# Moving 64-byte offsets from the moving to the stationary operand of 256-column products

## The chip, the cores and the metric

The kernel runs on one core of one Trainium2 chip. The metric is the device time of one execution in microseconds, as the median of several runs. A profile is one more execution, recorded by the hardware profiler.

## The reference, cut to what matters

The reference is three transformer layers on a sequence of 256 rows of width 1024, all in float32: a layer with two kinds of windowed attention, a layer with retention, each followed by a feed-forward block, and a hybrid layer with three attention branches.

```python
def _mlp(x, norm_g, w1, w2):                       # w1 [1024, 4096], w2 [4096, 1024]
    h = _rmsnorm(x, norm_g)
    return jnp.square(jax.nn.relu(h @ w1)) @ w2
...
a = jnp.einsum('bhid,bhjd->bhij', qc, kc) * dmask      # retention, 8 heads of 128
o = jnp.einsum('bhij,bhjv->bhiv', a, vc) + ...
```

## The kernel before

Every large product is done in float32r, split in two parts: an operand is hi + lo, and a product is three TensorE products, hi times hi, hi times lo and lo times hi (`mm3`, or three calls of `mm`). A TensorE product loads a stationary operand of 128 columns (LDWEIGHTS, the engine row PEld) and then streams a moving operand through it. Products whose moving operand has 512 columns are those of `panel` (a block of activations stationary, 512 columns of weights moving), of `proj` and of `mlp_out`. Products with 256 moving columns are of three kinds:

- `panel_T`, the first half of a feed-forward block: 128 columns of weights are stationary (`wh[:, fs]`, `wl[:, fs]`), all 256 rows of the transposed input xT move (`xh[:, k, :]`, `xl[:, k, :]`). A panel is 96 such products (4 blocks of 128 columns, 8 blocks of depth, 3 parts); there are 8 panels in each of the two feed-forward stages.
- the 16 heads of the first mixer (`even_head`): the values va or vb are stationary, the probabilities ph and pl move.
- the 8 heads of the retention mixer (`head` in `_odd`): for the scores the keys are stationary and the queries move; for the output the decayed scores ah and al are stationary and the values vv move.

Weights stream from memory all the time. SyncE's queue brings blocks of 1 MB into `raw`, ScalarE rounds half a block to `whi` (`w_hi`), VectorE subtracts to get `wlo` (`w_lo`); both are rings of WB = 5 buffers in the pool `wp`, used for all weights in order. A planner (`drive`) with modelled costs decides the order in which the tasks' instructions are written out; a half may be split at most LOOK = 3 halves ahead of the one in use. All tiles that TensorE reads lie at multiples of 512 bytes, with one exception: in the feed-forward stages the tile xT begins 64 bytes later (`xT_tiles(16)`, 16 floats). In the other stages xT is at a multiple of 512 bytes as well (`xT_tiles()`).

The pools of a stage are opened when the stage begins and given back at its end, so that the next stage's tiles lie where those of the last lay. The pool `wp` stands through the whole kernel.

Of the kernel before, what the change touches and what calls it, by code (L numbers as in the profile page):

```python
# [8 lines left out]
F32 = mybir.dt.float32  # L9
F32R = mybir.dt.float32r  # L10
# [5 lines left out]
P = 128  # L16
S = 256
D = 1024
NT = 2
# [18 lines left out]
def vap(ap, dims):  # L38

    return bass.AP(ap.tensor, ap.offset, [ap.ap[0]] + [list(d) for d in dims])  # L40


class Pools:

    def __init__(self, tc, ctx, name):
        self.lines = ctx.enter_context(tc.tile_pool(name=name, bufs=1))
        self.rest = ctx.enter_context(tc.tile_pool(name=name + "_s", bufs=1))

    def tile(self, shape, dt, **kw):
        n = 4
        for d in shape[1:]:
            n *= d
        return (self.rest if n % 512 else self.lines).tile(shape, dt, **kw)


class Task:
# [6 lines left out]
class Kernel:  # L65
# [25 lines left out]
    def __init__(self, ctx, tc, aps, taps=None):  # L91
        self.tc, self.nc, self.aps, self.ctx = tc, tc.nc, aps, ctx
        self.smallp = ctx.enter_context(tc.tile_pool(name="small", bufs=1))
        self.smallp.tile([P, PAD], F32, name="pad")
        self.mainp = ctx.enter_context(tc.tile_pool(name="main", bufs=1))
        self.wp = ctx.enter_context(tc.tile_pool(name="wp", bufs=1))
        self.wp.tile([P, 128 - 32], F32, name="padw")
        self.ps = ctx.enter_context(tc.tile_pool(name="ps", bufs=1, space=PSUM))
        self.now = 0.0
        self.free = {"T": 0.0, "A": 0.0, "V": 0.0, "P": 0.0, "D": 0.0}  # L100
        self.ready, self.used, self.touch = {}, {}, {}
        self.tasks, self.seq, self.cur = [], 0, None
        self.res = {}
        self.banks = [0.0] * 8
        self.ev = {}


    def spawn(self, gen, delay=0.0, prio=1):
# [311 lines left out]
    def w_parts(self, n):  # L420

        w = self.wseq[n // 2][1]
        return [slice(0, w), slice(w, 2 * w)] if n < self.FINE else [slice(0, 2 * w)]

    def w_hi(self):
        for n in range(2 * len(self.wseq)):
            self.cur.prio = lambda: self.w_prio(n, 2.3)
            yield ("if", lambda: n < len(self.wfree) + self.WB and n <= self.hcur + self.LOOK and n // 2 in self.wraw)
            if n >= self.WB:
                yield ("at", self.wfree[n - self.WB])  # L430
            m = 2 * self.wseq[n // 2][1]
            raw = self.wraw[n // 2][:, (n % 2) * m:(n % 2 + 1) * m]
            hi = self.wp.tile([P, 1024], F32R, name="whi", tag="whi", bufs=self.WB)
            self.whi[n] = hi
            for i, c in enumerate(self.w_parts(n)):
                yield from self.act(hi[:, c], raw[:, c], AF.Copy)
                self.fire(("hi", n, i))

    def w_lo(self):
        for n in range(2 * len(self.wseq)):  # L440
            self.cur.prio = lambda: self.w_prio(n, 1.3)
            yield ("ev", ("hi", n, 0))
            m = 2 * self.wseq[n // 2][1]
            raw = self.wraw[n // 2][:, (n % 2) * m:(n % 2 + 1) * m]
            hi = self.whi[n]
            lo = self.wp.tile([P, 1024], F32R, name="wlo", tag="wlo", bufs=self.WB)
            self.whalf[n] = (hi, lo)
            parts = self.w_parts(n)
            for i, c in enumerate(parts):
                yield ("ev", ("hi", n, i))  # L450
                t = yield from self.vtt(lo[:, c], raw[:, c], hi[:, c].bitcast(F32), ALU.subtract)
                self.fire(("w", n, i))
            if len(parts) == 1:
                self.fire(("w", n, 1))
            if n % 2 == 1:
                del self.wraw[n // 2]
                self.rawfree.append(t)
                self.w_dma()
# [155 lines left out]
            yield from post(t, ms)  # L614
        return [ss[0], ss[1], [], [], fin]

    def xT_tiles(self, at=0):

        xT = self.mainp.tile([P, 16 * S + 32], F32R, name="xT", tag="xT", bufs=1)
        return [xT[:, at + i * 8 * S:at + (i + 1) * 8 * S].rearrange("p (k q) -> p k q", k=8) for i in range(2)]  # L620


    def heads_T(self, src, dst, t, key, scale=1.0):
# [13 lines left out]
    def split_T(self, src, hi, lo, k0, t, key, scale=None):  # L637

        n = src.shape[1] // P
        yield ("rdy", src)  # L640
        yield ("acq", "bank", 1)
        ps = self.bank()
        yield ("op", "T", [], [src])
        for i in range(n):
            self.transpose(ps[:, i * P:(i + 1) * P], src[:, i * P:(i + 1) * P])
        pv = ps[:, :n * P].rearrange("p (i q) -> p i q", i=n)
        tk = slice(t * P, (t + 1) * P)
        end = yield from self.split(hi[:, k0:k0 + n, tk], lo[:, k0:k0 + n, tk], pv, scale)
        self.done(ps)
        self.fire(key, at=end)  # L650

# [215 lines left out]
    def _even(self, pool):  # L867
# [61 lines left out]

        qTa = pool.tile([P, 4, S], F32, name="qTa", tag="qTa")  # L930
        kTa = pool.tile([P, 1, S], F32, name="kTa")
        va = [[pool.tile([P, 256], F32R, name=f"va{n}{t}") for n in "hl"] for t in range(NT)]


        def pads():
# [2 lines left out]
        self.spawn(pads(), 12.0, self.LOW)  # L938
        qTb = pool.tile([P, 4, S], F32, name="qTb", tag="qTb")
        kTb = pool.tile([P, 4, S], F32, name="kTb")  # L940
        vb = [[pool.tile([P, 768], F32R, name=f"vb{n}{t}") for n in "hl"] for t in range(NT)]
        oT = [[pool.tile([P, 4, S], F32R, name=f"o{n}0") for n in "hl"], []]
        self.res["pT"], self.res["tab"] = 2, 2

# [111 lines left out]
    def mlp_input(self, i, gcol):  # L1056
        self.r2 = [None] * 2
        for t in range(NT):
            self.ev.pop(("r2", t), None)

        def post(t, ms):
            self.r2[t] = self.mt([P, 1], f"r2{t}", bufs=2)
            yield from self.vrecip(self.r2[t], ms)
            self.fire(("r2", t))
        self.st = self.stats(post)
        self.xT = self.xT_tiles(16)

    def mlp(self, i):
        with self.tc.tile_pool(name=f"mlp{i}", bufs=1) as pool:
            yield from self._mlp(pool, i)  # L1070

    def _mlp(self, pool, i):
        key = f"m{i}"
# [80 lines left out]
    def _odd(self, pool):  # L1154
# [6 lines left out]
        a, u, b, s2 = (scr[:, 16 * i:16 * i + 16] for i in range(4))  # L1161
# [20 lines left out]
        self.res["nat"] = 2  # L1182
        self.res["rhd"] = 2

        def qk_task(hp, qk):
            def task(t, ps):
                yield ("acq", "nat", 1)
                nat = pool.tile([P, 512], F32, name="nat", tag="nat", bufs=2)
                yield from self.act(nat, ps, AF.Copy)
                self.done(ps)  # L1190
                yield from self.split_T(nat, qk[0], qk[1], 0, t, ("rqk", hp, t))
                self.give("nat")
            return task

        def v_task(hp, vv):
            def task(t, ps):
                yield ("ev", ("st", "o", t))
                end = yield from self.split(vv[t][0], vv[t][1], ps, vs[t])
                self.done(ps)
                self.fire(("rv", hp, t), at=end)  # L1200
            return task
# [13 lines left out]
        def head(hp, hh, qk, vv, sg):  # L1215
# [3 lines left out]
            dt = pool.tile([P, 384], F32, name="dt", tag="dt", bufs=2)  # L1219
# [4 lines left out]
            ps = self.bank()  # L1224
            yield ("op", "T", [], [])
            for jt in range(2):
                js = slice(jt * P, (jt + 1) * P)
                self.mm3(ps[:, jt * S:(jt + 1) * S], qk[0][:, 2 + hh, js], qk[1][:, 2 + hh, js], qk[0][:, hh, :],
                         qk[1][:, hh, :], True, True)
            at = pool.tile([P, 512], F32, name="at", tag="at", bufs=2)  # L1230
            yield from self.vtt(at.rearrange("p (j i) -> p j i", j=2), ps.rearrange("p (j i) -> p j i", j=2),
                     vap(dt[:, P:P + S], [[-P, 2], [1, S]]), ALU.mult)
            self.done(ps)
            ah = pool.tile([P, 512], F32R, name="ah", tag="ah", bufs=2)
            al = pool.tile([P, 512], F32R, name="al", tag="al", bufs=2)
            yield from self.split(ah, al, at)
            yield ("rdy", al)
            yield ("ev", ("rv", hp, 0), ("rv", hp, 1))
# [47 lines left out]
            end = yield from self.split(uT[0][:, ks, :], uT[1][:, ks, :], un.rearrange("p (k q) -> p k q", k=2))  # L1286
# [6 lines left out]
        self.res["rset"] = 2  # L1293
        for hp in range(4):
            yield ("acq", "rset", 1)
            qk = [pool.tile([P, 4, S], F32R, name=n, tag=n, bufs=2) for n in ("qkh", "qkl")]
            vv = [[pool.tile([P, 512], F32R, name=n, tag=n, bufs=2) for n in (f"vh{t}", f"vl{t}")]
                  for t in range(NT)]
            sg = [pool.tile([P, 512], F32, name=f"sg{t}", tag=f"sg{t}", bufs=2) for t in range(NT)]
            yield from self.panel(self.xT, "xo", qk_task(hp, qk), tmajor=hp == 0)  # L1300
            for hh in range(2):
                self.spawn(head(hp, hh, qk, vv, sg), hh * 4.0)
            yield from self.panel(self.xT, "xo", v_task(hp, vv))
            yield from self.panel(self.xT, "xo", g_task(hp, sg))
# [446 lines left out]
```

## Time and profile before

| what | value |
|---|---|
| median of 3 runs | 1014.18 us (1013.54 to 1014.5) |
| the profiled execution | 1014.55 us, its span from first to last instruction 1012.8 us |
| TensorE (PE) busy | 1000.0 us, 5602 products |
| weight load (PEld) busy | 860.1 us |
| VectorE (DVE) busy | 689.5 us |
| ScalarE (ACT) busy | 536.1 us |
| granted TensorE clock, mean | 0.994 |

The span is the time from the first to the last instruction of the program; the 1.75 us beside it lie around them. A busy time is the union of an engine's instructions. Products are pipelined: a product's recorded duration is longer than the distance to the next product's start, so the cost of one product in a run is read from the starts, not from the durations.

### The profile page before, as it was taken

The page shows a single profiled execution, that of the slowest core. Times are in us where ns is not written, and L with a number is a line of the kernel's source. Part 1 is how long each engine was busy: PE and PEld are TensorE (multiplying, and loading weights), DVE is VectorE, ACT ScalarE, POOL GpSimd, SP SyncE. Part 2 cuts the span into 40 slices and gives each one's busy share as a digit, 9 for nine tenths or more (in the row PEclk, how much of TensorE's full clock was granted, in tenths as well). Part 3 has the DMA queues.
Part 4 walks back from the last instruction along what each step waited for, and adds up shares of the span by engine and source line. Part 5 has one row for each costly group of instructions (what it writes and reads, how often), then busy time and mean ns, then how long its engine had stood idle before and what let it go on. Part 6 is the DMA issues. An engine that isn't in the chain of part 4 may idle for free.

```text
span 1012.8 us, 14238 instructions
## 1 busy us (share of the span) xinstructions
PE 1000.0 (99%) x5602; PEld 860.1 (85%) x5602; DVE 689.5 (68%) x1133; ACT 536.1 (53%) x817; POOL 39.5 (4%) x44
## 2 busy tenths in 40 slices
PE   9989999999999999999999999999999999999997
PEld 7878889999998888888889999998878788888885
DVE  6997667555556977777667545556769756576774
ACT  7766646444445655656446444445554553454453
POOL 1340000000000000000000000000100000000000
PEclk9989999999999999999999999999999999999999
DMA  9734245555554544443545555553625435543531
GB/s 333 231 112 159 84 166 203 178 202 182 197 204 153 195 166 155 172 171 129 205 166 191 187 206 172 203 207 112 213 83 172 161 136 195 193 172 128 195 125 42
DMA packets 27108, 173.66 MB, mean 171 GB/s; under 512 B 3168, under 2 KB 3424, under 8 KB 7584
## 3 DMA queue, kind: packets, MB, share of 16 engines
q1 hardware_dynamic: 25344, 168.05, 47.2%
q0 software_dynamic: 1120, 4.06, 1.7%
q8 instruction: 44, 0.72, 0.3%
q10 hardware_dynamic: 576, 0.64, 0.2%
q14 instruction: 24, 0.20, 0.1%
HBM read 171.69 MB, written 1.05 MB: 171 GB/s over the span
## 4 chain that ended last, share of the span: by engine, by line
PE 95%; DVE 2%; DMA 1%; ACT 1%; issue 0%; POOLq 0%; ACTq 0%; DVEq 0%
PE bank L326 91%; PE bank L336 4%; DMA x<-in_x 1%; DVE p L273 1%; DVE tab L259 0%; DMA cols<-in_cols 0%; ACT p L246 0%; DVE pl L251 0%; DVE p L259 0%; DVE den L251 0%; DVE wlo L251 0%; DVE st L283 0%; DVE qn L251 0%; ACT whi L246 0%; ACT nraw L246 0%
## 5 line engine op out<-in xcount | busy, mean ns | idle before, releaser
L251 DVE TENSOR_TENSOR wlo<-raw,whi 128x1024 fp32r<-128x1024 f32 (+1 forms) x324 | 384.9, 1191 | 187.9 <-ACT whi L246 183.0
L246 ACT ACTIVATE whi<-raw 128x1024 fp32r<-128x1024 f32 (+1 forms) x324 | 333.3, 1032 | 239.5 <-PE bank L326 233.8
L326 PE MATMUL bank<-whi,xT 128*128 128x512 f32 (+2 forms) x1184 | 378.7, 390 | 0.7 <-ACT whi L246 0.4
L326 PEld LDWEIGHTS bank<-whi,xT 128*128 128x128 f32 x1184 | 221.1, 189 | 45.7 <-issue 3.0
L326 PE MATMUL bank<-wlo,xT 128*128 128x512 f32 (+2 forms) x592 | 227.1, 384 | 0.0
L326 PE MATMUL bank<-xT,whi 128*128 128x256 f32 x1024 | 182.1, 280 | 0.0
L326 PEld LDWEIGHTS bank<-xT,whi 128*128 128x128 f32 x1024 | 157.3, 187 | 1.1
L326 PE MATMUL bank<-xT,wlo 128*128 128x256 f32 x512 | 142.9, 279 | 0.0
L326 PEld LDWEIGHTS bank<-wlo,xT 128*128 128x128 f32 x592 | 112.0, 189 | 18.8
L326 PE MATMUL bank<-whi,hh 128*128 128x512 f32 x256 | 100.3, 392 | 0.0
L326 PE MATMUL bank<-whi,hl 128*128 128x512 f32 x256 | 99.8, 390 | 0.0
L326 PE MATMUL bank<-wlo,hh 128*128 128x512 f32 x256 | 99.6, 389 | 0.0
L326 PEld LDWEIGHTS bank<-xT,wlo 128*128 128x128 f32 x512 | 96.2, 188 | 0.0
L326 PEld LDWEIGHTS bank<-whi,hl 128*128 128x128 f32 x256 | 48.0, 188 | 10.4
L326 PEld LDWEIGHTS bank<-wlo,hh 128*128 128x128 f32 x256 | 48.1, 188 | 9.5
L326 PEld LDWEIGHTS bank<-whi,hh 128*128 128x128 f32 x256 | 48.1, 188 | 9.3
L246 ACT ACTIVATE p<-p,nm 128x256 f32<-128x256 f32 (+1 forms) x64 | 30.2, 473 | 27.1 <-DVE nm L273 26.9
L251 DVE TENSOR_TENSOR h<-h 128x512 f32<-128x512 f32 x32 | 22.0, 688 | 18.1 <-ACT h L246 18.1
L246 ACT ACTIVATE h<-bank 128x512 f32<-128x512 f32 x32 | 18.8, 587 | 28.6 <-PE bank L326 28.6
L246 ACT ACTIVATE hh<-h 128x512 fp32r<-128x512 f32 x32 | 20.2, 632 | 19.6 <-DVE h L251 19.6
L251 DVE TENSOR_TENSOR hl<-h,hh 128x512 fp32r<-128x512 f32 x32 | 22.0, 688 | 11.2 <-ACT hh L246 11.2
L326 PE MATMUL bank<-whi,uh 128*128 128x512 f32 x64 | 25.2, 393 | 0.0
(241 smaller groups left out, 1117.3 us busy)
## 6 DMA issues: line engine op xcount, KB each, us to landing
raw<-in_w_mlp_in SPq DMA_DIRECT2D x32, 1024.0 KB, 4.7
raw<-in_w_mlp_out SPq DMA_DIRECT2D x32, 1024.0 KB, 4.8
raw<-in_w_in SPq DMA_DIRECT2D x32, 1024.0 KB, 4.9
raw<-in_w_in_o SPq DMA_DIRECT2D x24, 1024.0 KB, 4.7
raw<-in_w_out_o SPq DMA_DIRECT2D x8, 1024.0 KB, 4.7
raw<-in_w_in_e SPq DMA_DIRECT2D x6, 1024.0 KB, 5.5
raw<-in_w_up SPq DMA_DIRECT2D x6, 1024.0 KB, 4.9
raw<-in_w_mem SPq DMA_DIRECT2D x4, 1024.0 KB, 4.8
```

The costliest lines, as they stand in the source:

```text
L246: self.nc.scalar.activation(out, in_, func, scale=scale, **kw)
L251: self.nc.vector.tensor_tensor(out, a, b, op=op)
L273: self.nc.vector.tensor_tensor_reduce(out, a, b, scale, init, op0, op1, acc)
L326: self.nc.tensor.matmul(out, lhsT, rhs, start=start, stop=stop, skip_group_check=shared)
L336: self.nc.tensor.transpose(out, in_, self.ident)
```

## The change

The 64 bytes are taken from the moving operand and given to the stationary one, in all three kinds of 256-column products:

- `xT_tiles` gives two tiles, each at a multiple of 512 bytes, in all stages.
- The weights of `w_mlp_in` get rings of their own (`mhi`, `mlo`, five buffers each, tiles of 1024 + 32 floats used from float 16 on) in a pool `mpool` that lives as long as the feed-forward stage. The weights of all other products, `w_mlp_out` among them, stay in `wp`. A half of `w_mlp_in` that is split before the stage has been opened still goes to `wp`.
- The values va and vb of the first mixer and the decayed scores ah and al of the retention mixer lie 64 bytes past a boundary (`half`), in a third pool `mid` of the mixer.
- In the retention mixer, queries and keys share a tile: the queries stay at its start, the keys begin at float 2 * 256 + 16 (`KO`).

The number of instructions of every engine and their shapes stay as they were.

```diff
+def halfway(pool, n, dt, **kw):
+    return pool.tile([P, n + 32], dt, **kw)[:, 16:16 + n]
...
+    def half(self, n, dt, **kw):
+        return halfway(self.mid, n, dt, **kw)
...
-        self.wp.tile([P, 128 - 32], F32, name="padw")
...
+    def w_tile(self, part, n):
+        if self.mpool and self.wseq[n // 2][0].startswith("w_mlp_in"):
+            return halfway(self.mpool, 1024, F32R, name="m" + part, tag="m" + part, bufs=self.WB)
+        return self.wp.tile([P, 1024], F32R, name="w" + part, tag="w" + part, bufs=self.WB)
...
-            hi = self.wp.tile([P, 1024], F32R, name="whi", tag="whi", bufs=self.WB)
+            hi = self.w_tile("hi", n)
...
-            lo = self.wp.tile([P, 1024], F32R, name="wlo", tag="wlo", bufs=self.WB)
+            lo = self.w_tile("lo", n)
...
-    def xT_tiles(self, at=0):
-        xT = self.mainp.tile([P, 16 * S + 32], F32R, name="xT", tag="xT", bufs=1)
-        return [xT[:, at + i * 8 * S:at + (i + 1) * 8 * S].rearrange("p (k q) -> p k q", k=8) for i in range(2)]
+    def xT_tiles(self):
+        return [self.mt([P, 8, S], n, F32R) for n in ("xh", "xl")]
...
-        va = [[pool.tile([P, 256], F32R, name=f"va{n}{t}") for n in "hl"] for t in range(NT)]
+        va = [[pool.half(256, F32R, name=f"va{n}{t}") for n in "hl"] for t in range(NT)]
...
-        vb = [[pool.tile([P, 768], F32R, name=f"vb{n}{t}") for n in "hl"] for t in range(NT)]
+        vb = [[pool.half(768, F32R, name=f"vb{n}{t}") for n in "hl"] for t in range(NT)]
...
-        self.xT = self.xT_tiles(16)
+        self.xT = self.xT_tiles()
...
-        with self.tc.tile_pool(name=f"mlp{i}", bufs=1) as pool:
+        with self.tc.tile_pool(name=f"mlp{i}", bufs=1) as pool, self.tc.tile_pool(name=f"mlp{i}_h", bufs=1) as self.mpool:
             yield from self._mlp(pool, i)
+        self.mpool = None
...
+        KO = 2 * S + 16
...
-                yield from self.split_T(nat, qk[0], qk[1], 0, t, ("rqk", hp, t))
+                yield from self.split_T(nat, *(vap(v[:, t * P:], [[KO, 2], [S, 2], [1, P]]) for v in qk), None, t,
+                                        ("rqk", hp, t))
...
-                self.mm3(ps[:, jt * S:(jt + 1) * S], qk[0][:, 2 + hh, js], qk[1][:, 2 + hh, js], qk[0][:, hh, :],
-                         qk[1][:, hh, :], True, True)
+                js = slice(KO + hh * S + jt * P, KO + hh * S + (jt + 1) * P)
+                qs = slice(hh * S, (hh + 1) * S)
+                self.mm3(ps[:, jt * S:(jt + 1) * S], qk[0][:, js], qk[1][:, js], qk[0][:, qs], qk[1][:, qs], True, True)
...
-            ah = pool.tile([P, 512], F32R, name="ah", tag="ah", bufs=2)
-            al = pool.tile([P, 512], F32R, name="al", tag="al", bufs=2)
+            ah = pool.half(512, F32R, name="ah", tag="ah", bufs=2)
+            al = pool.half(512, F32R, name="al", tag="al", bufs=2)
...
-            qk = [pool.tile([P, 4, S], F32R, name=n, tag=n, bufs=2) for n in ("qkh", "qkl")]
+            qk = [pool.mid.tile([P, 4 * S + 32], F32R, name=n, tag=n, bufs=2) for n in ("qkh", "qkl")]
```

## Rows read from the trace of the kernel before

**Rows 1.** The page: span, busy time of the engines, and the chain that ended last.
```profile
span 1012.8 us, 14238 instructions
...
PE 1000.0 (99%) x5602; PEld 860.1 (85%) x5602; DVE 689.5 (68%) x1133; ACT 536.1 (53%) x817; POOL 39.5 (4%) x44
...
PE 95%; DVE 2%; DMA 1%; ACT 1%; issue 0%; POOLq 0%; ACTq 0%; DVEq 0%
```

**Rows 2.** Windows: the two feed-forward stages; window, length, then busy (count) by engine.
```profile
150.40:319.80 169.40, 169.40 (x1112) 155.43 (x1112) 98.77 (x104) 84.38 (x99) 0.00 (x0) 1.00 0.54 189
...
531.00:700.80 169.80, 169.80 (x1114) 155.68 (x1113) 98.75 (x104) 84.33 (x99) 0.00 (x0) 1.00 0.54 187
```

**Rows 3.** Groups by form, TensorE: the 256-column products; count, busy us, mean ns.
```profile
L326 PE MATMUL bank<-xT,whi 128*128 128x256 f32 x1024 | 182.1, 280 | 0.0
...
L326 PE MATMUL bank<-xT,wlo 128*128 128x256 f32 x512 | 142.9, 279 | 0.0
...
L326 PE MATMUL bank<-vh,al 128*128 128x256 f32 x32 | 9.1, 283 | 0.0
...
L326 PE MATMUL bank<-ph,vah 128*128 128x256 f32 x16 | 4.7, 291 | 0.0
...
L326 PE MATMUL bank<-qkh,qkl 128*128 128x256 f32 x16 | 4.5, 283 | 0.0
```

**Rows 4.** Timeline, TensorE, first feed-forward stage: start us, duration us, what.
```profile
204.92 0.40 PE L326 MATMUL bank<-xT,whi 128*128 128x256 f32 x2
...
216.23 0.40 PE L326 MATMUL bank<-whi,hh 128*128 128x512 f32 x1
...
227.15 0.40 PE L326 MATMUL bank<-xT,whi 128*128 128x256 f32 x2
```

**Rows 5.** Timeline, TensorE, a retention head: 24 products with 256 columns between two with 512.
```profile
355.76 0.28 PE L326 MATMUL bank<-vh,ah 128*128 128x256 f32 x1
355.88 0.28 PE L326 MATMUL bank<-vl,ah 128*128 128x256 f32 x1
...
358.64 0.40 PE L326 MATMUL bank<-whi,xT 128*128 128x512 f32 x1
```

**Rows 6.** Timeline, TensorE, a head of the first mixer: 12 products after a 512-column one.
```profile
48.49 0.28 PE L326 MATMUL bank<-ph,vah 128*128 128x256 f32 x1
48.60 0.28 PE L326 MATMUL bank<-ph,val 128*128 128x256 f32 x1
...
49.80 0.28 PE L326 MATMUL bank<-pl,vah 128*128 128x256 f32 x1
```

**Rows 7.** Timeline, TensorE, another head of the first mixer, after transposes.
```profile
55.24 0.28 PE L326 MATMUL bank<-ph,val 128*128 128x256 f32 x1
...
55.72 0.28 PE L326 MATMUL bank<-pl,vah 128*128 128x256 f32 x1
```

**Rows 8.** Timeline, TensorE, products with 512 columns in the feed-forward stage (20 between).
```profile
200.16 0.39 PE L326 MATMUL bank<-whi,hh 128*128 128x512 f32 x1
...
204.69 0.39 PE L326 MATMUL bank<-whi,hl 128*128 128x512 f32 x1
```

**Rows 9.** Timeline, TensorE, products with 328 columns (9 from first to last row).
```profile
723.33 0.46 PE L326 MATMUL bank<-whi,xT 128*128 128x328 f32 x2
...
724.68 0.31 PE L326 MATMUL bank<-whi,xT 128*128 128x328 f32 x1
```

**Rows 10.** Timeline and group, TensorE: bfloat16 products with 256 columns at the start.
```profile
5.68 1.91 PE L831 MATMUL bank<-vx 128*128 128x256 bf16 x16
...
L831 PE MATMUL bank<-vx 128*128 128x256 bf16 x15 | 1.8, 272 | 0.0
```

**Rows 11.** Groups by form, weight loads, 356.1 to 358.5 us and 207.1 to 215 us.
```profile
L326 PEld LDWEIGHTS bank<-vh,ah 128*128 128x128 f32 x7 | 1.3, 192 | 0.0
...
L326 PEld LDWEIGHTS bank<-xT,whi 128*128 128x128 f32 x46 | 7.0, 187 | 0.0
```

**Rows 12.** Timeline around the entry of the first feed-forward stage, ScalarE and TensorE.
```profile
147.98 1.05 ACT L246 ACTIVATE whi<-raw 128x1024 fp32r<-128x1024 f32 x1
...
150.54 1.04 ACT L246 ACTIVATE whi<-raw 128x1024 fp32r<-128x1024 f32 x1
...
148.06 0.39 PE L326 MATMUL bank<-whi,o 128*128 128x512 f32 x1
```

**Rows 13.** Writers of xT, 140 to 152 us, then 320 to 338 us: ns min/median/max.
```profile
L251 DVE TENSOR_TENSOR xT<-nraw,xT x3: 684/685/685, 144.3 to 151.0; 128x512 fp32r<-128x512 f32 x3
...
L251 DVE TENSOR_TENSOR xT<-nraw,xT x4: 681/686/689, 322.8 to 333.1; 128x512 fp32r<-128x512 f32 x4
```

More of the change, by code (lines that the diff above doesn't have):

```diff
@@ L48, in __init__ @@
         self.lines = ctx.enter_context(tc.tile_pool(name=name, bufs=1))
+        self.mid = ctx.enter_context(tc.tile_pool(name=name + "_h", bufs=1))
         self.rest = ctx.enter_context(tc.tile_pool(name=name + "_s", bufs=1))
@@ L645, in split_T @@
             self.transpose(ps[:, i * P:(i + 1) * P], src[:, i * P:(i + 1) * P])
-        pv = ps[:, :n * P].rearrange("p (i q) -> p i q", i=n)
-        tk = slice(t * P, (t + 1) * P)
-        end = yield from self.split(hi[:, k0:k0 + n, tk], lo[:, k0:k0 + n, tk], pv, scale)
+        if k0 is None:
+            pv = ps[:, :n * P].rearrange("p (a b q) -> p a b q", a=2, b=n // 2)
+        else:
+            pv = ps[:, :n * P].rearrange("p (i q) -> p i q", i=n)
+            hi, lo = (v[:, k0:k0 + n, t * P:(t + 1) * P] for v in (hi, lo))
+        end = yield from self.split(hi, lo, pv, scale)
         self.done(ps)
@@ L1065, in mlp_input @@
         self.st = self.stats(post)
-        self.xT = self.xT_tiles(16)
+        self.xT = self.xT_tiles()
     def mlp(self, i):
-        with self.tc.tile_pool(name=f"mlp{i}", bufs=1) as pool:
+        with self.tc.tile_pool(name=f"mlp{i}", bufs=1) as pool, self.tc.tile_pool(name=f"mlp{i}_h", bufs=1) as self.mpool:
             yield from self._mlp(pool, i)
+        self.mpool = None
     def _mlp(self, pool, i):
@@ L1226, in head @@
             for jt in range(2):
-                js = slice(jt * P, (jt + 1) * P)
-                self.mm3(ps[:, jt * S:(jt + 1) * S], qk[0][:, 2 + hh, js], qk[1][:, 2 + hh, js], qk[0][:, hh, :],
-                         qk[1][:, hh, :], True, True)
+                js = slice(KO + hh * S + jt * P, KO + hh * S + (jt + 1) * P)
+                qs = slice(hh * S, (hh + 1) * S)
+                self.mm3(ps[:, jt * S:(jt + 1) * S], qk[0][:, js], qk[1][:, js], qk[0][:, qs], qk[1][:, qs], True, True)
             at = pool.tile([P, 512], F32, name="at", tag="at", bufs=2)
```

## The prediction

> **What bounds the kernel now.** I read the page first: TensorE is busy 1000.0 of 1012.8 us and the chain that ended last runs over it for 95% [rows 1]. VectorE and ScalarE are a third and a half idle. So time comes only from making TensorE's own products start closer together, or is lost by making it wait. [...]
>
> What one product costs can't be read from the recorded durations (280 ns each [rows 3], far more than their share of the stage), so I went to the starts in the timeline. In a feed-forward stage a panel of 96 products with 256 columns goes from 204.92 to 216.23 us, 11.31 us or 117.8 ns each, and the 48 products of 512 columns behind it take until 227.15, 10.92 us or 227 ns each [rows 4]. [...] So the two stages hold 1536 products at 117.8 ns, 181 us in all.
>
> These 117.8 ns are those of an xT that begins 64 bytes past a boundary while the weights lie on one. Where both operands lie on one, 256 columns cost more: in a retention head 23 products take 2.76 us, 120.0 ns each [rows 5]; in a head of the first mixer ten take 1.20 us, 120 ns [rows 6]. Two other readings show that this is not the array's own pace. The first product of the run in rows 6 takes only 0.11 us. And 20 products of 512 columns take 4.53 us, 226.5 ns each [rows 8], so that half of one is 113.3 ns.
>
> [...] And the load itself is longer where the pitch is: 192 ns recorded at 120 ns, 187 at 117.8 [rows 11]. [...]
>
> [...]
>
> **The change part by part.**
>
> The weights of panel_T go to +64, xT back to 0. No row has a stationary operand off a boundary, so the cost is bounded by neighbours. [...] Above: the offset of xT is given up and the stationary's brings nothing, 120.0 ns [rows 5]; if the load's reading itself became longer by the 5 ns between its two durations [rows 11], 122.8 ns. Between stand 117.8 ns (only the relation of the two counts, and it is again half a period of 128 bytes) and 113.3 ns, the first product of rows 6 and half a 512-column product. I take 113.3 ns. [...] This is an inference from neighbours, not a row.
>
> Not all products get it. The halves of w_mlp_in that are split before the stage is opened still lie in wp, on a boundary, and xT now too. The rows of the entry show the whi at 147.98 us written just as the last output product starts at 148.06, and the next at 150.54 [rows 12]; so two or three of the first panel's four halves, 24 products each, say 60 products a stage. They cost 120.0 instead of 117.8: 120 x 2.2 ns = +0.3 us. The other 1416: 1416 x (117.8 - 113.3) ns = -6.4 us.
>
> The mixers: 96 products in the retention outputs (three forms of 32), 48 in its scores (three of 16), 96 in the first mixer (six of 16) [rows 3]. From 120 to 113.3 ns is 1.6 us; the first of each run has the short step already, so I take -1.2 us, with 0 and -2.6 (at 109.2) as ends.
>
> The rings of their own for w_mlp_in: the same instructions in the same number, no DMA added and none moved; the queue of SyncE waits on raw as before. Looser reuse can't help an engine that never waits in these stages. The new pool lies where the mixer's tiles lay, so its first ScalarE write waits until the last output product has read: 148.06 plus 0.39 us against 147.98 [rows 12], half a microsecond on ScalarE. Behind it on that queue is the next xT part and the next whi; the fourth half is first used after 48 products of the panel, 48 x 117.8 ns = 5.7 us behind that last output product, so this is hidden; uncovered it would cost 0.5 us a stage. Writing 64 bytes past a boundary costs VectorE nothing: the same 685 and 686 ns for xT with and without the offset [rows 13].
>
> Sum: -6.4 + 0.3 - 1.2 = -7.3 us. The profiled execution took 1014.55 us, 1012.8 of it span; it becomes 1007.2, and the median, 0.4 below the profiled one, 1006.9.
>
> **The rivals.**
>
> No change that counts. If only the distance between the two operands modulo 128 bytes matters, moving one by 64 is the same as moving the other: the panels stay at 117.8 ns, the mixers go from 120 to 117.8 (-0.5 us), the early halves cost +0.3: 1014.0 us. For it: half a period is the same seen from either side. Against it: the short first products show that the order in time counts as well. [...]
>
> Slower. What helped in rows 4 was where the moving stream begins, not how the two stand; then the panels fall back to 120.0 ns, 1536 x 2.2 = +3.4 us, mixers unchanged: 1017.6. It decides as soon as the panels' pitch passes 119.1 ns, +2.0 us. For it: the only offset row there is moves the stream. [...] At 122.8 ns it would be +7.7 us, 1021.9.
>
> Wait at the entries: 0.5 us in each stage if the cover were gone, 1 us; it decides nothing alone.
>
> **How the numbers follow.** About 0.2%, 2.0 us, is what a measurement of this kernel tells from no change. Faster, with a pitch between 109.2 and 116.7 ns: 0.50. No change that counts: 0.29. Slower: 0.21, of which 0.16 at 120 ns and the rest above or by a wait. The likeliest, 1007, has its own range of 1003 to 1011 (a pitch of 111 to 116 ns). The range over all reaches up to 1017.8, past the 120 ns case, and down to 1003; beyond it lie a pitch near 109 and the 122.8 ns case, under 2 in 10 together.
>
> **What would show it.** In the timeline a panel of 96 products should take 10.9 us where it took 11.31 (11.5 in the slower case), the window of each feed-forward stage should be 166 us or a little more, and the weight loads of panels and heads should be at 187 ns or below. In the first panel of a stage two or three halves named wlo and whi should still run at 120. Heads: 12 products in 1.36 us instead of 1.44. The 512-column products should stay at 227 ns; if they move, a base address has shifted and my reading of the addresses is wrong. A new wait of TensorE for whi at a stage's entry would be the pool's.

## The result and the profile after

The changed kernel takes 1007.84 us (median of 4 runs, 1006.9 to 1008.24), the kernel before 1013.86 us (4 runs beside them, 1013.2 to 1014.5). The ratio is 0.9939, 95% interval 0.9922 to 0.9957: 6.0 us faster. The profiled execution took 1007.6 us.

The lines move by nine: L326 of before is L335. The page of the kernel after, for [rows 1]; TensorE still does everything that counts:

```profile
span 1005.8 us, 14188 instructions
...
PE 992.7 (99%) x5602; PEld 853.9 (85%) x5602; DVE 682.6 (68%) x1133; ACT 526.1 (52%) x817; POOL 39.6 (4%) x44
...
PE 95%; DVE 2%; DMA 1%; ACT 1%; issue 0%; SPq 0%; POOLq 0%; DVEq 0%
```

The fixed windows of [rows 2] no longer cover the same work, so here are the two feed-forward stages from their first 256-column product to the start of the product behind the last output product. Columns: window, length, then busy time (count) of PE, PEld, DVE, ACT, POOL, the granted clock, the DMA share, GB/s. The kernel after:

```profile
147.46:324.16 176.70, 176.70 (x1169) 161.36 (x1168) 103.11 (x114) 85.69 (x109) 0.00 (x0) 1.00 0.50 186
524.86:701.56 176.70, 176.70 (x1169) 161.36 (x1168) 103.13 (x114) 85.69 (x109) 0.00 (x0) 1.00 0.50 182
```

The same stages of the kernel before, cut at the same products:

```profile
148.28:327.90 179.62, 179.62 (x1170) 164.17 (x1169) 106.55 (x114) 90.47 (x109) 0.00 (x0) 1.00 0.53 183
528.85:708.47 179.62, 179.62 (x1169) 164.15 (x1168) 106.52 (x114) 90.43 (x109) 0.00 (x0) 1.00 0.52 179
```

Each stage is 2.92 us shorter, 5.84 of the 7.0 us between the two spans. TensorE is busy in all of both windows and the granted clock is 1.00 in both, so neither a wait nor the clock has changed. Of the rest, 0.82 us lie ahead of the first stage, 0.26 between the two (from the start of the last output product of the one to the first 256-column product of the other 201.18 us became 200.92) and 0.09 behind the second. The 0.82 us can't be put down to the change: bench and entry below run the program of the kernel after up to there, and in them the first stage begins at 147.56 and 146.71 us, against 147.46.

A panel and the 48 output products behind it, kernel after, timeline of TensorE, for [rows 4]:

```profile
203.31 0.28 PE L335 MATMUL bank<-xh,mhi 128*128 128x256 f32 x1
...
214.20 0.40 PE L335 MATMUL bank<-whi,hh 128*128 128x512 f32 x1
...
225.11 0.28 PE L335 MATMUL bank<-xh,mhi 128*128 128x256 f32 x1
```

The 96 products take 10.89 us, 113.4 ns each, where they took 11.31; the 48 with 512 columns still take 10.91, 227 ns. The groups by form, for [rows 3], and the loads of one panel (205 to 213 us), for [rows 11]:

```profile
L335 PE MATMUL bank<-xh,mhi 128*128 128x256 f32 x464 | 128.2, 276 | 0.0
...
L335 PE MATMUL bank<-xh,whi 128*128 128x256 f32 x48 | 13.9, 289 | 0.0
...
L335 PEld LDWEIGHTS bank<-xh,mhi 128*128 128x128 f32 x24 | 4.5, 188 | 0.0
```

With the two other forms that is 3 x 464 = 1392 products from the new rings and 3 x 48 = 144, three halves a stage, from the old ones. Those go at 120.0 ns, as 36 products of the first panel show (4.32 us); the last row is the first product from the new ring:

```profile
150.35 0.28 PE L335 MATMUL bank<-xh,wlo 128*128 128x256 f32 x1
...
154.67 0.28 PE L335 MATMUL bank<-xh,wlo 128*128 128x256 f32 x1
154.78 0.28 PE L335 MATMUL bank<-xh,mhi 128*128 128x256 f32 x1
```

The entry, for [rows 12]: ScalarE waits 0.43 us for TensorE before its first write to the new pool, and TensorE waits for nothing there.

```profile
147.66 1.06 ACT L255 ACTIVATE mhi<-raw 128x1024 fp32r<-128x1024 f32 x1 [0.43 <-PE bank L335]
```

The heads, for [rows 5, 6]. A retention head of 24 products, from its first to the 512-column product behind it, takes 2.83 us, 117.9 ns each and not 113.3:

```profile
351.99 0.28 PE L335 MATMUL bank<-vh,ah 128*128 128x256 f32 x1
...
354.82 0.40 PE L335 MATMUL bank<-whi,xh 128*128 128x512 f32 x1
```

In the first mixer eleven products take 1.25 us, 114 ns each; the first two steps are 117 and 116 ns, the others 113 or 114:

```profile
48.96 0.28 PE L335 MATMUL bank<-ph,vah 128*128 128x256 f32 x1
49.08 0.28 PE L335 MATMUL bank<-ph,val 128*128 128x256 f32 x1
...
50.22 0.28 PE L335 MATMUL bank<-pl,vah 128*128 128x256 f32 x1
```

### The profile page after: what moved, and what is told of

Same layout as the page of the kernel before. It is cut to its first block, busy times and chain, and to the rows that moved or that the text cites. A ratio compares the mean times of both kernels' runs of the same rounds, so it can differ in the third digit from the quotient of the medians.

```text
span 1005.8 us, 14188 instructions
## 1 busy us (share of the span) xinstructions
PE 992.7 (99%) x5602; PEld 853.9 (85%) x5602; DVE 682.6 (68%) x1133; ACT 526.1 (52%) x817; POOL 39.6 (4%) x44
## 4 chain that ended last, share of the span: by engine, by line
PE 95%; DVE 2%; DMA 1%; ACT 1%; issue 0%; SPq 0%; POOLq 0%; DVEq 0%
PE bank L335 91%; PE bank L345 4%; DMA x<-in_x 1%; DVE p L282 1%; DVE tab L268 0%; DMA const<-in_const 0%; ACT p L255 0%; DVE pl L260 0%; DVE p L268 0%; DVE den L260 0%; DVE wlo L260 0%; DVE st L292 0%; DVE qn L260 0%; ACT whi L255 0%; SPq L397 0%
## 5 line engine op out<-in xcount | busy, mean ns | idle before, releaser
L260 DVE TENSOR_TENSOR wlo<-raw,whi 128x1024 fp32r<-128x1024 f32 (+2 forms) x266 | 311.5, 1182 | 90.6 <-ACT whi L255 88.7
L255 ACT ACTIVATE whi<-raw 128x1024 fp32r<-128x1024 f32 (+2 forms) x266 | 268.7, 1023 | 135.3 <-PE bank L335 130.4
L335 PE MATMUL bank<-whi,xh 128*128 128x512 f32 (+2 forms) x592 | 232.1, 395 | 0.0
L335 PE MATMUL bank<-whi,xl 128*128 128x512 f32 (+2 forms) x592 | 226.7, 383 | 0.0
L335 PE MATMUL bank<-wlo,xh 128*128 128x512 f32 (+2 forms) x592 | 226.6, 383 | 0.0
L335 PEld LDWEIGHTS bank<-whi,xh 128*128 128x128 f32 x592 | 111.6, 189 | 22.2 <-issue 3.0
L335 PEld LDWEIGHTS bank<-whi,xl 128*128 128x128 f32 x592 | 111.4, 188 | 22.1
L335 PE MATMUL bank<-xh,mlo 128*128 128x256 f32 x464 | 128.2, 276 | 0.0
L335 PE MATMUL bank<-xh,mhi 128*128 128x256 f32 x464 | 128.2, 276 | 0.0
L335 PE MATMUL bank<-xl,mhi 128*128 128x256 f32 x464 | 128.2, 276 | 0.0
L335 PEld LDWEIGHTS bank<-wlo,xh 128*128 128x128 f32 x592 | 111.7, 189 | 18.7
L335 PE MATMUL bank<-whi,hh 128*128 128x512 f32 x256 | 100.2, 391 | 0.0
L335 PE MATMUL bank<-wlo,hh 128*128 128x512 f32 x256 | 99.8, 390 | 0.0
L335 PE MATMUL bank<-whi,hl 128*128 128x512 f32 x256 | 99.7, 389 | 0.0
L335 PEld LDWEIGHTS bank<-xh,mhi 128*128 128x128 f32 x464 | 87.1, 188 | 0.5
L335 PEld LDWEIGHTS bank<-xl,mhi 128*128 128x128 f32 x464 | 87.1, 188 | 0.4
L335 PEld LDWEIGHTS bank<-xh,mlo 128*128 128x128 f32 x464 | 87.1, 188 | 0.0
L335 PEld LDWEIGHTS bank<-whi,hl 128*128 128x128 f32 x256 | 48.1, 188 | 10.2
```

The source lines that it names most:

```text
L255: self.nc.scalar.activation(out, in_, func, scale=scale, **kw)
L260: self.nc.vector.tensor_tensor(out, a, b, op=op)
L335: self.nc.tensor.matmul(out, lhsT, rhs, start=start, stop=stop, skip_group_check=shared)
```

## Experiments

The two kinds of head set the question. Both got 64 bytes, one runs near the pace forecast (114 ns in the first mixer) and one does not (117.9 in retention). The addresses in the two built programs differ in one thing that the diff does not name. A buffer of 1024 + 32 floats is 4224 bytes, 33 x 128. So neighbours in a ring stand in turn 64 and 192 bytes past a multiple of 256, and as the lo ring lies five buffers behind the hi ring (21,120 bytes, 165 x 128), hi and lo of one half always stand 128 bytes apart modulo 256. The values va and vb (288 and 800 floats, 9 x 128 and 25 x 128 bytes, one buffer each) are also 128 apart between hi and lo. For ah and al (two buffers of 2176 bytes) and the keys (two of 4224) the distance is a multiple of 256: one class. So theory A: the pace of 113.3 ns comes from the half line together with the distance of 128 between hi and lo. Theory B is the prediction's: a stream that begins on a boundary and a stationary operand half a line off are enough. (Here and in the expectations, line is a word for addresses alone: a line is 128 bytes, whole lines begin at a multiple of 128, half a line off is 64 bytes past one.)

**one_class: the feed-forward rings without the distance.**

```diff
-            return halfway(self.mpool, 1024, F32R, name="m" + part, tag="m" + part, bufs=self.WB)
+            return self.mpool.tile([P, 1024 + 64], F32R, name="m" + part, tag="m" + part, bufs=self.WB)[:, 16:16 + 1024]
```

> The changed kernel with the rings of w_mlp_in widened by another 128 bytes a buffer, so that hi and lo of every half lie at 64 bytes past a multiple of 256 and no longer 128 apart modulo 256. Theory A: the panels fall back to 117.8 ns, 1392 products x 4.3 ns = +6 us against the changed kernel, about 1014 us. Theory B: modulo 128 nothing has changed, 113.5 ns and about 1008 us.

Measured: 1013.38 us (1012.6 to 1013.99, 10 runs), ratio 0.999 (0.9981 to 1.0) to the kernel before. Timeline, the same panel:

```profile
204.27 0.28 PE L335 MATMUL bank<-xh,mhi 128*128 128x256 f32 x1
...
215.57 0.40 PE L335 MATMUL bank<-whi,hh 128*128 128x512 f32 x1
...
226.48 0.28 PE L335 MATMUL bank<-xh,mhi 128*128 128x256 f32 x1
```

The panel is back at 11.30 us, 117.7 ns. Every weight still begins 64 bytes past a 128-byte boundary, and the gain is gone. B falls, for the sequence that the kernel has.

**mixer_stagger: the distance given to the retention heads.** The kernel after with 32 floats between the rings of ah and al and between those of qkh and qkl:

```diff
+            pool.mid.tile([P, 32], F32R, name="pada", tag="pada", bufs=1)
...
+            pool.mid.tile([P, 32], F32R, name="padq", tag="padq", bufs=1)
...
```

> The changed kernel with 128 bytes between the buffers of ah and al and between those of the two query and key tiles. Theory A: the 96 retention outputs, at 117.8 ns in the changed kernel, run at 113.3; in the scores the moving queries of qkl are shifted as well as its keys, so that load and stream stay 64 apart, and they stay at 117.8. Theory B: no change, 117.8 ns in both. The time moves by less than 0.7 us either way, within what can be told; the pitch in the trace decides.

Measured: 1007.27 us (1006.25 to 1008.22, 4 runs), ratio 0.9935 (0.992 to 0.9949). A retention head in the timeline:

```profile
352.97 0.28 PE L335 MATMUL bank<-vh,ah 128*128 128x256 f32 x1
...
355.70 0.40 PE L335 MATMUL bank<-whi,xh 128*128 128x512 f32 x1
```

24 products in 2.73 us, 113.8 ns, from 117.9. One_class had also taken away that neighbours in a ring stand 128 bytes apart. That is not the cause: the neighbours of ah stand so in the kernel after too (2176 bytes are 17 x 128), and only the distance between hi and lo is new here. The scores, whose moving query ql shifts by 128 as well, stay at a mean of 117.9 ns (steps of 112 to 124). Against the kernel after the time is the same within both intervals. 96 products at 4 ns less are 0.4 us, and the stretch between the two feed-forward stages is shorter by just that, 200.51 us for 200.92.

**before_stagger: only the distance, in the kernel before.** xT stays 64 bytes off, and the common rings of wp get buffers of 1056 floats, so that hi and lo stand 128 apart:

```diff
-        self.wp.tile([P, 128 - 32], F32, name="padw")
+        self.wp.tile([P, 32], F32, name="padw")
...
-            hi = self.wp.tile([P, 1024], F32R, name="whi", tag="whi", bufs=self.WB)
+            hi = self.wp.tile([P, 1024 + 32], F32R, name="whi", tag="whi", bufs=self.WB)[:, :1024]
...
-            lo = self.wp.tile([P, 1024], F32R, name="wlo", tag="wlo", bufs=self.WB)
+            lo = self.wp.tile([P, 1024 + 32], F32R, name="wlo", tag="wlo", bufs=self.WB)[:, :1024]
```

> The kernel before (xT 64 bytes off, weights on boundaries, one ring for all weights) with each buffer of the weight rings 128 bytes longer, so that whi and wlo of a half differ by 128 modulo 256. No stationary operand is 64 bytes past a 128-byte boundary. Theory A: the panels run at 113.3 ns all the same, 1536 x 4.5 = -6.9 us, about 1007 us. Theory B: modulo 128 nothing has changed, 117.8 ns, 1014 us.

Measured: slower, 1018.56 us (1016.91 to 1019.13, 4 runs), ratio 1.0043 (1.0026 to 1.006). The timeline shows why:

```profile
204.79 0.39 PE L326 MATMUL bank<-xT,whi 128*128 128x256 f32 x2
...
215.80 0.39 PE L326 MATMUL bank<-whi,hh 128*128 128x512 f32 x1
...
226.88 0.40 PE L326 MATMUL bank<-xT,whi 128*128 128x256 f32 x2
```

The panel gains, 11.01 us, 114.7 ns. But the 48 output products take 11.08 us, 230.8 ns, where they took 10.92. The expectation had not counted that: over the whole kernel the 2713 of them that follow one another directly rise from a mean of 227.8 to 231.2 ns, +9.2 us, while 1514 steps in the panels fall from 117.8 to 114.3 ns, -5.3 us. The sum, +3.9, is nearly the 4.6 us measured. This is what the rings of their own do in the change: they keep the distance away from the 512-column products, in which the weights are the moving operand, and these stay at 227 ns there.

**bench: the offsets by themselves.** Behind the last output of the kernel after, runs of 36 products hi x a, hi x b, lo x a, first all with 256 columns, then all with 512. The kernel ahead of them is unchanged.

```diff
...
+            def run(n, m, a, b, count=12):
+                ma, mb = (v[:, :n] for v in mov[m])
+                for _ in range(count):
+                    for s, v in ((st[a][0], ma), (st[a][0], mb), (st[b][1], ma)):
+                        nc.tensor.matmul(ps[:, :n], s, v, start=True, stop=True)
...
```

> The changed kernel with a measurement behind its last output: 16 runs of 36 products with 256 moving columns and 16 with 512, in triples hi, hi, lo as in the panels, each run with its own start addresses (bytes past a multiple of 256) of the stream and of the hi and lo stationary operands. The output is that of the changed kernel; the time grows by some 215 us. Theory A (the place of the load against the stream modulo 256 bytes, and whether hi and lo differ by 128): stream 0 with 0/0 120.0 ns; 64/64 and 192/192 117.8; 64/192 and 192/64 113.3; stream 64 with 0/0 117.8, with 0/128 113.3. Theory B (the prediction's: modulo 128, the stationary operand half a line off and the stream on whole lines): 64/64, 192/192 and 64/192 all 113.3; stream 64 with 0/128 stays at 117.8. Neither says what 32, 96 or 16 bytes do, nor whether runs of 512 columns leave 226.7 ns.

Measured, mean distance of starts over the last 24 products of a run, in ns (offsets of the stream, hi and lo in bytes past a multiple of 256; 10 of the 16 runs of each width):

| stream, hi, lo | 256 columns | 512 columns |
|---|---|---|
| 0, 0, 0 | 120.0 | 226.7 |
| 0, 0, 128 | 119.3 | 231.1 |
| 0, 128, 128 | 120.0 | 232.6 |
| 0, 64, 64 | 113.3 | 233.3 |
| 0, 64, 192 | 113.3 | 232.0 |
| 64, 0, 0 | 113.3 | 233.3 |
| 64, 0, 128 | 113.3 | 233.3 |
| 64, 64, 192 | 119.3 | 231.3 |
| 0, 32, 32 | 118.3 | 233.3 |
| 0, 96, 224 | 117.8 | 233.3 |

Two of these runs in the timeline, each by its first product and the first of the run behind it:

```profile
1027.99 0.28 PE L856 MATMUL bank<-m0a,hi0x 128*128 128x256 f32 x1
...
1032.31 0.28 PE L856 MATMUL bank<-m0a,hi0x 128*128 128x256 f32 x1
...
1040.93 0.28 PE L856 MATMUL bank<-m0a,hi64x 128*128 128x256 f32 x1
...
1045.02 0.28 PE L856 MATMUL bank<-m0a,hi192x 128*128 128x256 f32 x1
```

36 products in 4.32 us, 120.0 ns, and in 4.09, 113.6. With half a line between stream and stationary the runs came to 113.3 ns, whichever of the two was moved, and both moved is none (119.3). But A did not hold here: one class, 64 and 64, went at 113.3 ns, where one_class had 117.7 with the same offsets. Something besides the addresses decided. With 512 columns each offset tried cost 4 to 8 ns, 128 bytes too; both on a multiple of 256 was the best. Each offset ran once, in one order, so these figures hold for what went ahead of each here.

**entry: what goes ahead, or how the addresses step.** In the kernel a panel comes behind products of 512 columns on boundaries and steps through its weights; in bench it came behind other 256-column runs with fixed addresses. C1: what went ahead decides. C2: the stepping does. Behind the last output again, each run led in by 18 products of 512 columns on boundaries:

```diff
...
+            for m, a, b in ((0, 64, 64), (0, 64, 192), (64, 0, 0), (64, 0, 128), (0, 0, 0)):
+                run(512, 0, 0, 0, 6)
+                run(256, m, a, b)
+            for m, a, b in ((0, 64, 64), (0, 64, 192), (64, 0, 0), (64, 0, 128), (0, 0, 0)):
+                run(512, 0, 0, 0, 6)
+                panel(m, a, b, False)
+            run(256, 0, 64, 192)
+            panel(0, 64, 64, False)
+            run(512, 0, 0, 0, 6)
+            panel(0, 64, 64, True)
```

> The changed kernel with a second measurement behind its last output, longer by some 130 us. In the first one, runs with hi and lo in one class (64/64, and stream 64 with 0/0) went at 113.3 ns, where the panels of the kernel before and of the widened rings go at 117.8 with the same classes. Two explanations. C1, the entry: the state of the two reads when a run begins decides, and a panel begins behind 512-column products; then runs at fixed addresses behind six triples of 512-column products go at 117.8 ns for 64/64 and for stream 64 with 0/0, and at 113.3 for 64/192 and for stream 64 with 0/128. C2, the steps: a panel moves to another block of weights and of xT with each triple; then the runs at fixed addresses go at 113.3 in all four classes, and only those that step through addresses as a panel does go at 117.8 for 64/64 and stream 64 with 0/0. With both operands on a boundary 120 ns in each.

Measured, timeline of three stepping panels of 72 products, each up to the product behind it: offsets 0, 64, 64 behind 512 columns; 0, 64, 192 behind 512 columns; and 0, 64, 64 behind a run of 64 and 192 (1142.52 to 1147.97) that already went at 113.3:

```profile
1083.76 0.28 PE L866 MATMUL bank<-m0a,hi64x 128*128 128x256 f32 x1
...
1092.24 0.40 PE L856 MATMUL bank<-m0a,hi0x 128*128 128x512 f32 x1
...
1096.35 0.28 PE L866 MATMUL bank<-m0a,hi64x 128*128 128x256 f32 x1
...
1104.53 0.40 PE L856 MATMUL bank<-m0a,hi0x 128*128 128x512 f32 x1
...
1147.97 0.28 PE L866 MATMUL bank<-m0a,hi64x 128*128 128x256 f32 x1
...
1156.13 0.40 PE L856 MATMUL bank<-m0a,hi0x 128*128 128x512 f32 x1
```

8.48 us, 117.8 ns; 8.18 us, 113.6; 8.16 us, 113.3. The first and the third are the same products on the same addresses. The last panel, 64 and 64 behind 512 columns once more (its outputs go to two banks), steps at 117.8 ns again, so the place in the program is not the cause. Fixed addresses behind 512 columns gave the same as stepping ones (117.8 for 64 and 64, 113.3 for 64 and 192), so C2 falls and C1 stands: products 64 and 64 have two steady paces, what went ahead decides which, and the distance of 128 between hi and lo leads from the 512-column products into the faster one. One expectation was missed: the stream moved and hi and lo 128 apart (64, 0, 128) stayed at 118.9 ns in both forms, where bench had shown 113.3.

**moved_stream and stagger_only: the halves of the cause in the kernel.** Both keep the rings of 1056 floats, used from their start (hi and lo 128 apart, no half line); moved_stream moves xT by 64 bytes as the kernel before does, stagger_only leaves it on a boundary (the last two lines are those of moved_stream alone).

```diff
-            return halfway(self.mpool, 1024, F32R, name="m" + part, tag="m" + part, bufs=self.WB)
+            return self.mpool.tile([P, 1024 + 32], F32R, name="m" + part, tag="m" + part, bufs=self.WB)[:, :1024]
...
-        self.xT = self.xT_tiles()
+        self.xT = self.xT_tiles(16)
```

> The changed kernel with the 64 bytes of the feed-forward stages given back to xT: rings of their own for w_mlp_in with buffers 128 bytes longer, but used from their start. Theory A: only the relation counts and the stagger of 128 between hi and lo; the panels go at 113.5 ns, the 512-column products stay at 227 since the shared rings are untouched, about 1008 us (the early halves at 117.8 instead of 120, -0.3). Theory B: it is the stationary operand that must be off the boundary; 117.8 ns and about 1014 us.

Measured: 1009.45 us (median of four runs, 1008.97 to 1010.78; a fifth, 2840.8 us, is left out), ratio 0.9957 (0.9941 to 0.9973).

```profile
203.60 0.40 PE L336 MATMUL bank<-xT,mhi 128*128 128x256 f32 x2
...
214.53 0.39 PE L336 MATMUL bank<-whi,hh 128*128 128x512 f32 x1
```

This panel takes 10.93 us, 113.9 ns. Others have stretches at 117 to 124 and take up to 116.6 ns a product, and the mean over all is 115.5 ns, against 114.1 in the kernel after, the early halves included in both. Most of the gain comes with the stream moved too, but it is less steady.

> The changed kernel without the 64 bytes in the feed-forward stages: xT on a boundary, rings of their own for w_mlp_in with buffers 128 bytes longer, used from their start. Theory A, with the first measurement's run of 0/128: 119.3 ns, 1392 products x 5.8 = +8 us against the changed kernel, about 1016 us. Rival: the stagger or the separate rings alone make the gain: 113.5 ns and 1008 us.

Measured: 1015.3 us (1014.13 to 1016.26, 10 runs), ratio 1.0013 (1.0003 to 1.0022).

```profile
204.67 0.29 PE L335 MATMUL bank<-xh,mhi 128*128 128x256 f32 x1
...
216.06 0.40 PE L335 MATMUL bank<-whi,hh 128*128 128x512 f32 x1
```

11.39 us, 118.6 ns. The rings of their own and the distance bring nothing over the kernel before without the half line.

**mlp_only and mixers_only: the change in two parts.** The first is the kernel after with va, vb, ah, al and the keys on boundaries again (`pool.tile`, and the first two lines below); the second is the kernel after with all weights in wp (the last line), xT moved by 64 bytes and the pad of wp as before.

```diff
-        KO = 2 * S + 16
+        KO = 2 * S
...
-            return halfway(self.mpool, 1024, F32R, name="m" + part, tag="m" + part, bufs=self.WB)
...
```

> The feed-forward part of the change alone: va, vb, ah, al and the keys lie on boundaries again, as in the kernel before. By what the trace of after shows, the panels keep 113.3 to 113.5 ns: 1392 products x (117.8 - 113.5) = -6.0 us, the 144 early products at 120.0 instead of 117.8 = +0.3, together -5.7 us, ratio 0.9944; heads at 120 as before. The sum of the prediction would give -6.1 us for this part. If the mixers carry more than the trace lets see, it stays above -5 us.

Measured: 1007.81 us (1007.32 to 1008.42, 5 runs), ratio 0.9936 (0.9924 to 0.9949): the whole of the gain.

> The mixers' part alone: feed-forward stages as before (xT 64 bytes past, weights in wp). By the trace of after: 96 products of the first mixer at about 115 ns instead of 120 and 144 of retention at 117.8 instead of 120: -0.5 -0.3 = -0.8 us, ratio 0.9992. The prediction's 113.3 ns for all of them gave -1.2 us, 0.9988. The two differ by less than a timing of the whole kernel tells; the pitches in the trace decide: retention outputs at 117.8 (hi and lo 256 bytes apart) or 113.3 ns.

Measured: 1013.33 us (1012.57 to 1014.14, 11 runs), ratio 0.9991 (0.9982 to 1.0). Its retention outputs have a mean of 117.9 ns, the value for one class. The stretch between the two feed-forward stages is 200.92 us in this kernel, as in the kernel after and 0.26 less than before: that is all that 144 retention products bring. What the heads of the first mixer bring can't be read from the start of the first stage. With the heads changed it is 0.12 us earlier (148.28 became 148.16) or 0.23 (147.69 in mlp_only, 147.46 in the kernel after), but the kernel after, bench and entry, the same up to there, differ by 0.85. Their steps allow an estimate: the mean of the 81 steps from one such product straight to the next fell from 118.7 ns to 115.3, over 96 products 0.3 us.

## Why the prediction was right, and where its reason was not

The time was right, 1006.9 to 1007 forecast and 1007.84 measured (a gain of 7.3 us forecast, 6.0 between the medians), and so was the term that carries it, the panels'. The reason given for that term was wrong. A side effect of the diff that the prediction had not seen made the number true, and that was luck.

- **Panels, -6.4 us.** The pace taken was 113.3 ns; 113.4 was measured in the panel. With the early halves the prediction had -6.1 us for the two stages, the windows show -5.84. It had 120 early products, there are 144; the 24 more cost 24 x 6.6 = 0.16 us.
- **The reason for 113.3 ns: the stationary operand 64 bytes off, the stream back on a boundary.** By its own word an inference from neighbours. This step failed: it is not enough in this kernel. Theory B is that step, and one_class is exactly it: the stationary operand half a line off, the stream on a boundary, and 117.7 ns. In bench a stream off the boundary did as well as a stationary operand off it (113.3 ns both). The first rival, that only the relation modulo 128 bytes matters, was right about the offset itself: it forecast 1014.0 us, and one_class took 1013.38. What the prediction did not work out is the size of the new buffers: 33 x 128 bytes, five of them, set hi and lo 128 bytes apart modulo 256. With that and the half line the panels behind 512-column products take 113.4 ns, without the distance 117.7 (one_class), without the half line 118.6 (stagger_only), and in entry the two sets of addresses take 113.6 and 117.8.
- **The two readings behind that reason.** Half of a 512-column product is 113.3 ns [rows 8], but no run links the two: in bench offsets of 0, 0, 0 gave 120.0 ns with 256 columns and 226.7 with 512, and 0, 64, 64 gave 113.3 and 233.3; in neither is the one half of the other. The step of 0.11 us in [rows 6] was the first of its run, and bench shows that the pace with both on a boundary settles at 120.0. [Rows 7] has no such step: four products in 0.48 us are 120 ns each, the slow pace. But the sentence that the order in time counts as well was borne out: entry has one set of addresses at two paces (113.3 and 117.8 ns).
- **The end of 109.2 ns for the mixers and the chances.** No run shows it for float32r: it is the distance of bfloat16 products, 15 steps in 1.91 - 0.272 us [rows 10]. The shortest pace of the float32r products with 256 columns in the panels and runs read here is 113.3 ns (bench, entry).
- **Early halves at 120.0 ns.** Right; three halves a stage.
- **Mixers, -1.2 us.** Mis-sized. The 144 products of retention went to 117.8 ns, not 113.3, and gave 0.26 us; the heads of the first mixer, with hi and lo 128 apart, went to a mean of 115.3 ns, by estimate 0.3 us. No part of it shows in a timing: mlp_only equals the kernel after.
- **The wait at the entry.** Right, with the size: 0.43 us on ScalarE for 0.5 forecast, and TensorE did not wait.
- **512-column products.** At 227 ns as forecast. With one ring for all weights and hi and lo 128 bytes apart they took 230.8 ns (before_stagger).
- **Loads at 187 ns or below.** This sign says nothing: 188 ns at 113.4 ns a product ([rows 11] has 187 at 117.8). The recorded length of a load does not tell these two paces apart; at 120.0 it is 192, before and after.
- **One shape, three paces.** At a granted clock of 1.00 float32r products with 256 columns took 113.4 ns in the panel after, 117.8 in the panel before and 120.0 in the early halves after, by the addresses and, as entry shows (8.16 and 8.48 us for one set), by what went ahead.

What stays open: why the distance of 128 bytes leads from the 512-column products into the faster pace, and why the moved stream (64, 0, 128) reaches it in bench, for most of moved_stream, and not in entry. Bench had one order of runs, so what the other offsets do behind 512 columns is open too. No run shows whether the weight load has a part in the paces. No version is measurably better than the kernel after; mixer_stagger's median is 0.6 us lower, within the spread of both, though its trace has the 0.4 us.

## What to carry to other kernels

Where products follow one another without a wait, look at the distance of their starts and at the addresses of all operands, of one product and of its neighbours: here moving a 64-byte offset from one operand to the other was worth nothing by itself (117.7 for 117.8 ns) and 4 ns a product together with 128 bytes between the hi and the lo part. Padding a buffer changes the place of every buffer behind it, so work the new addresses out before saying what an offset does. An offset that helps one shape can cost another (before_stagger: 3.5 ns less with 256 columns, 3.4 more with 512): give the shapes separate buffers, and time a product in the sequence in which it stands, since a measurement by itself can settle at another pace (offsets of 0, 64, 64: 113.3 ns in bench, 117.7 in one_class).

## What the runs showed of the hardware that was not expected

- The same float32r products with 256 columns on the same addresses run steadily at 113.3 or at 117.8 ns, by what ran ahead of them (entry: 72 products in 8.16 or 8.48 us).
- With 256 columns 64 bytes modulo 128 between stream and stationary operand gave 113.3 ns in bench where 0 gave 120.0, either operand moved; offsets of 16, 32 and 96 bytes gave 117.8 to 118.8.
- With 512 columns it is the other way round: 226.7 ns in bench with both on a multiple of 256 bytes, 231.1 to 234.3 with any offset tried, 128 bytes among them. With hi and lo 128 bytes apart as moving operands, the products of a whole kernel rise from a mean of 227.8 to 231.2 ns (before_stagger).
